# Turning token tiles once between an output projection and the FFN's up projection

## The chip, the cores and the metric

The kernel runs on one core of a Trainium2 chip. The metric is the device time of one execution in microseconds, the median of several runs. The core has five engines that run side by side and meet by semaphores: TensorE (PE in the profile; PEld is its weight load), VectorE (DVE), ScalarE (ACT), GpSimd (POOL) and SyncE (SP), whose queue issues most DMA transfers. Matmuls write to PSUM, which holds eight banks of 128 x 512 float32 numbers; VectorE and ScalarE read it, GpSimd works in SBUF.

## The reference

A trunk of two layers over 1024 tokens with 1024 features. Layer 0 mixes tokens by differential attention, layer 1 by multi-head latent attention; after each comes a gated MLP whose up projection passes through a causal convolution.

```python
for i in range(DEPTH):
    h = rms_norm(x, attn_norm_g[i])
    if i % N_MIXERS == 0:
        x = x + diff_attention(h, ...)      # ends in  o @ w_o
    else:
        x = x + mla_attention(h, ...)       # ends in  o @ w_o
    h = rms_norm(x, ffn_norm_g[i])
    x = x + conv_ffn(h, ffn_w_up[i], ffn_conv_w[i], ffn_conv_b[i], ffn_w_down[i])
return rms_norm(x, final_norm_g)

def conv_ffn(h, w_up, conv_w, conv_b, w_down):
    u = h @ w_up                            # 1024 x 5632
    c = causal depthwise conv of width 3 over u, plus conv_b
    g, val = jnp.split(c, 2, axis=-1)
    return (jax.nn.silu(g) * val) @ w_down
```

What matters here is the seam in each layer: `x + o @ w_o`, the norm of the sum, and the operands of `h @ w_up`.

## The kernel before

**Products in two parts.** Every float32 operand is split into an upper part in the fp32r format (`hi`, a ScalarE copy, line 127) and the remainder (`lo`, a subtraction on VectorE or GpSimd, line 130). A product is three matmuls (`mm3`, lines 119 to 121): upper by lower, upper by upper, lower by upper.

**Seven products instead of eight.** The up projection multiplies 2 x 2 blocks by a Strassen-Winograd scheme. For pair q the token tiles q and q + 4 give four blocks. B11 and B21 are the first and second feature halves of tile q, B12 and B22 those of tile q + 4. The scheme needs B11, B21, B22 and the sums T1 = B12 - B11, T2 = B22 - T1, T3 = B22 - B12 and T4 = B21 - T2. Weights have blocks A11, A12, A22 and sums S1 to S4. All seven token operands are needed with features on the partitions, so they are turned: four TensorE transposes of 128 x 128 into a PSUM bank (line 186), then an upper and a lower part read that bank (`turn_blocks`).

**The seam, `project_rest` (from line 623).** Eight token tiles come in the order 0, 4, 1, 5, 2, 6, 3, 7. Each tile multiplies the second half of the attention's output (loaded from DRAM by `project`, line 589, and split) with `w_o` into two PSUM banks, tag S, first 512 columns and then the rest, 24 matmuls each. VectorE adds the product to the tile (line 698), SP stores the sum for the later residual (`x_d`, line 699), ScalarE sums the squares (line 157), VectorE and GpSimd form the reciprocal root (lines 164, 167), and VectorE applies it and the gain in place (line 657), so this step also waits until the store has read the tile. The sums T1 to T4 are taken in token layout, mostly on GpSimd (lines 634 to 641), and turned afterwards like the blocks. `half` places the turns in the middle of a tile's matmuls, two tiles after the tile that they turn. What is left after tile 7 goes into the list `late`: one entry before each of the first products.

**The first products, in `up` (from line 748).** For the first of the 22 feature blocks, the products run on token halves of 256 columns in the order of `FIRST`: 14 products of 12 matmuls. `ORDER0` names the operands: A11 B11, A12 B21, S1 T1, S4 B22, S2 T2, S3 T3, A22 T4. Weight sums are made by `sum_of` (line 775), parts by `high`, `low` and `prepare`. Results wait in PSUM banks and are added up on VectorE (lines 864 to 874) and copied on ScalarE (line 862). From the second block on, products have 512 columns.

**What sets the order.** Inside `manual_schedule` the named engines run in the order in which the program is written: PE and DVE through the seam and the first products, ACT too from there on. All other queues (ACT, POOL and SP in the seam) are ordered by a planner that simulates the program. PSUM has two double banks (tag S), three single banks (tag b) and one (tag u). `halves(...)`, `units(...)` and `slots(...)` name places of 2, 4 and 8 KB per partition in SBUF.

Of the kernel before, what the change touches and what calls it, by code (L numbers as in the profile page):

```python
# [13 lines left out]
ALU = mybir.AluOpType  # L14
# [42 lines left out]
class Trunk:  # L57
# [526 lines left out]
    def project(self, i, ks, W, o_d, os, raw):  # L584

        nc = self.nc
        s = slice(i * P, (i + 1) * P)
        o = raw([P, 4, P])
        nc.sync.dma_start(o, o_d[ks[0] : ks[0] + 4, :, s].rearrange("k p s -> p k s"))
        oh, ol = (os([P, 4, P], F32R) for _ in range(2))  # L590
        self.hi(oh, o)
        self.lo(ol, o, oh, nc.gpsimd)
# [5 lines left out]
        return into  # L598

# [23 lines left out]
    def project_rest(self, W, o_d, os, X, at, x_d, g, junk, places, nat, more, begin):  # L623

        nc = self.nc
        T = {}
        sums = {}
        first, rest = slice(0, 512), slice(512, 1024)

        def sub(name, q, eng):  # L630
            a, b = (X[i] for i in self.PAIRS[q])
            if name == "T1":
                sums[q] = nat([P, 512])
                eng.tensor_sub(sums[q], b[:, first], a[:, first])
            elif name == "T2":
                eng.tensor_sub(sums[q], b[:, rest], sums[q])
            elif name == "T4":
                eng.tensor_sub(sums[q], a[:, rest], sums[q])
            else:
                sums["T3", q] = more([P, 512])  # L640
                eng.tensor_sub(sums["T3", q], b[:, rest], b[:, first])

        def turn(name, q):

            if name not in T:
                T[name] = [self.at(place, [P, 4, 512], F32R) for place in places[name]]
            a, b = (X[i] for i in self.PAIRS[q])
            src = {"B11": a[:, first], "B21": a[:, rest], "B22": b[:, rest], "T3": sums.get(("T3", q))}.get(name)
            if src is None:
                src = sums[q]  # L650
            s = slice(q * P, (q + 1) * P)
            self.turn_blocks(src, lambda part: T[name][part][:, :, s])

        v, gp = nc.vector, nc.gpsimd

        def norm(i):
            nc.vector.scalar_tensor_tensor(X[i], X[i], r.pop(i), g, ALU.mult, ALU.mult)
            if i >= 4:
                sub("T1", i - 4, v if i == 7 else gp)

        def turns(*which):
            for x in which:
                turn(*x)

        def half(n):

            if n < 2:
                return
            i = tiles[n - 2]
            q = i % 4  # L670
            if i < 4:
                turns(("B11", q), ("B21", q))
                if q:
                    turns(("B22", q - 1))
            else:
                turns(("T1", q))
                sub("T2", q, gp)
                if q == 0:
                    sub("T3", q, gp)

        tiles = [i for pair in self.PAIRS for i in pair]
        r = {}
        ready = self.project(tiles[0], range(4, 8), W, o_d, os, self.raw)
        region = ExitStack()
        region.enter_context(self.tc.manual_schedule(engines={mybir.EngineType.PE, mybir.EngineType.DVE}))
        for n, i in enumerate(tiles):
            into, y = ready, self.big()
            into(y[:, :512], 0)
            half(n)
            if n + 1 < NT:  # L690
                ready = self.project(tiles[n + 1], range(4, 8), W, o_d, os, self.raw)
            into(y[:, 512:], 512)
            if n == NT - 1:
                begin()
# [35 lines left out]

# [1212 lines left out]
```

## Time and profile before

| | |
|---|---|
| median of 3 runs | 2436.9 us (2436.48 to 2437.53) |
| span of the profiled execution | 2437.8 us |
| TensorE busy | 2366.7 us, 97% |
| VectorE busy | 1904.5 us, 78% |
| ScalarE busy | 1304.2 us, 53% |
| GpSimd busy | 628.4 us, 26% |
| seam and first products, layer 0 | 546.4 to 619.2 us |
| seam and first products, layer 1 | 1733.5 to 1808.2 us |

The profile shows one execution. No time is recorded for it beside its span, which stands 0.9 us above the median. Busy time of overlapping matmuls is counted once, and their ends are modelled. In rows of the timeline stand start, duration, engine, line, operation, output and inputs by name, and in brackets the idle time before and what ended it. In rows of the waits view stand who waited for whom, the total, the count and the longest. A "group" row has count, busy time and the mean in ns. The two rows of the table on the seam begin with the first matmul of the third token tile and end with the first product of 512 columns.

### The profile page before, as it was taken

To read this page: it belongs to the slowest core of one execution; us is meant where nothing else is said; L and a number is where in the kernel's file an instruction comes from. 1 tells how busy PE (TensorE), PEld (TensorE's weight loads), DVE (VectorE), ACT (ScalarE), POOL (GpSimd) and SP (SyncE) were. 2 spreads that over 40 slices of the span, in tenths; PEclk is the share of its full clock that TensorE was granted. 3 is DMA by queue.
4 is the path that set the end of the run, shared out by engine and by line. 5 is a ranking of instruction groups with operands and counts; after the bars stand their busy time and mean duration, and the time that the engine had idled before them with its cause. 6 is when DMAs were issued, how large, how long until landed. Compare 5 with 4: busy or idle time off the path is not lost. (4 is left out here: it accounts for less than half of the span.)

```text
span 2437.8 us, 32825 instructions
## 1 busy us (share of the span) xinstructions
PE 2366.7 (97%) x12032; PEld 2010.7 (82%) x12032; DVE 1904.5 (78%) x3094; ACT 1304.2 (53%) x2434; POOL 628.4 (26%) x500
## 2 busy tenths in 40 slices
PE   7999999999999999999999999999999999999998
PEld 6888787888888888878898789988888888887886
DVE  6667776856888888899864788886478888888997
ACT  5677777844444444444444777775344444443444
POOL 4545454425000000000042666664330000000001
PEclk9999999999999999999999999999999999999999
DMA  4101101233222222553222111123312222227502
GB/s 161 44 33 42 35 36 44 100 100 126 70 78 82 83 82 91 199 171 116 84 89 61 62 40 40 40 88 109 104 70 87 80 93 79 78 86 276 169 5 78
DMA packets 95793, 213.93 MB, mean 88 GB/s; under 512 B 8720, under 2 KB 33936, under 8 KB 95632
## 3 DMA queue, kind: packets, MB, share of 16 engines
q1 hardware_dynamic: 86448, 184.04, 22.5%
q10 hardware_dynamic: 9184, 27.79, 3.1%
q8 instruction: 95, 1.56, 0.3%
q14 instruction: 66, 0.54, 0.1%
HBM read 159.37 MB, written 52.43 MB: 87 GB/s over the span
## 5 line engine op out<-in xcount | busy, mean ns | idle before, releaser
L167 POOL TENSOR_TENSOR st<-st,mhalf 128x1 f32<-128x1 f32 x56 | 36.2, 648 | 1315.7 <-DVE st L164 1310.7
L127 ACT CAST u<-h 128x512 fp32r<-128x512 f32 (+2 forms) x242 | 146.0, 619 | 279.7 <-DVE h L775 259.8
L119 PE MATMUL S<-s,u 128*128 128x512 f32 (+1 forms) x752 | 286.1, 380 | 0.6 <-DVE s L130 0.5
L120 PE MATMUL S<-s,u 128*128 128x512 f32 (+1 forms) x752 | 284.5, 378 | 0.0
L121 PE MATMUL S<-s,u 128*128 128x512 f32 (+1 forms) x752 | 284.5, 378 | 0.0
L119 PE MATMUL b<-s,u 128*128 128x512 f32 x588 | 230.6, 392 | 2.1 <-DVE S L1631 1.0
L121 PE MATMUL b<-s,u 128*128 128x512 f32 x588 | 229.0, 390 | 0.0
L120 PE MATMUL b<-s,u 128*128 128x512 f32 x588 | 229.0, 389 | 0.0
L832 DVE SCALAR_TENSOR_TENSOR u<-u,conv,u 128x1023 f32<-128x1023 f32 (+1 forms) x176 | 224.8, 1277 | 1.9 <-ACT u L828 1.9
L149 POOL TENSOR_TENSOR u<-u,st 128x384 f32<-128x384 f32 (+7 forms) x160 | 169.6, 1070 | 149.2 <-DVE st L1639 107.2
L119 PE MATMUL u<-s,s 128*128 128x512 f32 (+1 forms) x440 | 177.9, 404 | 13.4 <-ACT h L556 7.1
L127 ACT CAST s<-u 128x512 fp32r<-128x512 f32 (+2 forms) x202 | 128.8, 673 | 103.4 <-PE u L121 37.6
L130 DVE TENSOR_TENSOR u<-b,u 128x512 fp32r<-128x512 f32 (+1 forms) x256 | 158.0, 630 | 29.6 <-ACT u L127 27.9
L121 PE MATMUL u<-s,s 128*128 128x512 f32 (+1 forms) x440 | 172.6, 392 | 0.0
L120 PE MATMUL u<-s,s 128*128 128x512 f32 (+1 forms) x440 | 172.2, 391 | 0.0
L119 PEld LDWEIGHTS S<-s,u 128*128 128x128 f32 x752 | 142.0, 189 | 27.7 <-DVE s L130 0.9
L120 PEld LDWEIGHTS S<-s,u 128*128 128x128 f32 x752 | 142.0, 189 | 26.3
L121 PEld LDWEIGHTS S<-s,u 128*128 128x128 f32 x752 | 141.9, 189 | 26.1
L127 ACT CAST u<-b 128x512 fp32r<-128x512 f32 (+1 forms) x256 | 133.6, 550 | 36.6 <-PE b L252 27.4
L835 ACT ACTIVATE u<-u 128x1024 f32<-128x1024 f32 x44 | 46.8, 1063 | 187.5 <-DVE u L832 187.5
L130 DVE TENSOR_TENSOR u<-h,u 128x512 fp32r<-128x512 f32 x166 | 114.1, 687 | 32.4 <-ACT u L127 31.5
L130 DVE TENSOR_TENSOR s<-u,s 128x512 fp32r<-128x512 f32 (+2 forms) x187 | 127.5, 715 | 12.0 <-ACT s L127 11.8
(263 smaller groups left out, 6645.3 us busy)
## 6 DMA issues: line engine op xcount, KB each, us to landing
u<-in_ffn_up SPq DMA_DIRECT2D x88, 512.0 KB, 3.9
g_d<-u ACTq DMA_DIRECT2D x44, 512.0 KB, 2.6
u<-in_ffn_down SPq DMA_DIRECT2D x66, 256.0 KB, 4.9
u<-g_d SPq DMA_DIRECT2D x62, 256.0 KB, 3.8
s<-in_da_wqkv SPq DMA_DIRECT2D x23, 512.0 KB, 3.2
x_d<-u SPq DMA_DIRECT2D x16, 512.0 KB, 2.9
s<-x_d SPq DMA_DIRECT2D x8, 1024.0 KB, 10.7
u<-o_d SPq DMA_DIRECT2D x24, 256.0 KB, 2.8
```

The costliest lines, as they stand in the source:

```text
L119: mm(out, lh, rl, start=first, stop=False, skip_group_check=onto)
L120: mm(out, lh, rh, start=False, stop=False, skip_group_check=onto)
L121: mm(out, ll, rh, start=False, stop=last, skip_group_check=onto)
L127: self.nc.scalar.copy(out, src)
L130: (eng or self.nc.vector).tensor_sub(out, src, hi.bitcast(F32))
L149: self.nc.gpsimd.tensor_mul(x, x, s.to_broadcast(list(x.shape)))
L167: nc.gpsimd.tensor_tensor(r, s, self.mhalf, ALU.pow)
L832: nc.vector.scalar_tensor_tensor(t[half][:, back:], u[half][:, : S - back], w, t[half][:, back:], ALU.mult, ALU.add)
L835: nc.scalar.activation(t[0], t[0], AF.Silu)
```

## The change

- Each token tile is turned once, in its two halves: 16 sets of four transposes per layer instead of 28. The turn of a tile stands at the start of the matmuls of the tile after the next, and no longer in the middle. Tile 3 is turned after tile 7's matmuls, tile 7 before the fourth of the first products.
- B12 stays as a turned block too. ScalarE copies it to SBUF, and T1 to T4 are taken in the turned layout by VectorE, from the PSUM banks of the blocks and from one another. T1 gets a place of its own, T2, T3 and T4 overwrite the normed tiles. Their upper and lower parts are made from SBUF. Lower parts of T1 are made on GpSimd, and of T2 where the text says `gp`.
- A tile's add, squares and norm follow one tile later in the order of the text, during the next tile's matmuls. Loads of the attention's output are issued two tiles ahead.
- Tile 7 is added, squared and normed in halves of 512 columns; the normed halves go to two places of their own (h12, h13).
- GpSimd runs in written order too, until the first products end. Weight parts of the first block are made at named points (`start.part`), the third on VectorE, the fourth lower part on GpSimd.
- The list `late` has parts instead of turns. The two layers differ in what is made early: `("T1",)` in layer 0, `("T1", "T2", "B22")` in layer 1.

```diff
-    def project(self, i, ks, W, o_d, os, raw):
...
+    def project_load(self, i, ks, o_d, raw):
+        o = raw([P, 4, P])
         s = slice(i * P, (i + 1) * P)
+        self.nc.sync.dma_start(o, o_d[ks[0] : ks[0] + 4, :, s].rearrange("k p s -> p k s"))
+        return o
+
+    def project_parts(self, o, ks, W, os):
+        oh, ol = (os([P, 4, P], F32R) for _ in range(2))
+        self.hi(oh, o)
+        self.lo(ol, o, oh, self.nc.gpsimd)
...
-    def project_rest(self, W, o_d, os, X, at, x_d, g, junk, places, nat, more, begin):
+    def project_rest(self, W, o_d, os, X, at, x_d, g, junk, places, sums, early, begin):
...
+        def turn(i):
+            names = ("B11", "B21") if i < 4 else ("B12", "B22")
+            for name, cols in zip(names, (first, rest)):
+                ps = banks[name, i % 4] = self.bank("u" if name == "B22" else "b")
+                x = normed(i, cols)
+                for k in range(4):
+                    nc.tensor.transpose(ps[:, k * P : (k + 1) * P], x[:, k * P : (k + 1) * P], self.ident)
...
+        def copy(q):
+            tmp["B12", q] = sums([P, 512])
+            nc.scalar.copy(tmp["B12", q], banks["B12", q])
+
+        def sub(name, q):
+            x, y = {
+                "T1": lambda: (tmp["B12", q], banks["B11", q]),
+                "T3": lambda: (banks["B22", q], tmp["B12", q]),
+                "T2": lambda: (banks["B22", q], tmp["T1", q]),
+                "T4": lambda: (banks["B21", q], tmp["T2", q]),
+            }[name]()
+            if name == "T1":
+                tmp[name, q] = sums([P, 512])
+            else:
+                tmp[name, q] = normed(*{"T2": (q, first), "T3": (q + 4, first), "T4": (q + 4, rest)}[name])
+            dve.tensor_sub(tmp[name, q], x, y)
...
+        outer.enter_context(self.tc.manual_schedule(engines={mybir.EngineType.PE, mybir.EngineType.DVE}))
+        inner.enter_context(self.tc.manual_schedule(engines={mybir.EngineType.Pool}))
         for n, i in enumerate(tiles):
+            into, ys[n] = ready, self.big()
+            before = tiles[n - 1] if n else None
+            older = tiles[n - 2] if n > 1 else None
+            if older is not None:
+                q, a_tile = older % 4, older < 4
+                turn(older)
+            into(ys[n][:, first], 0)
+            into(ys[n][:, rest], 512)
+            load(n + 2)
+            if n + 1 < NT:
+                ready = parts(n + 1)
+            else:
+                start = begin()
+            if before is None:
+                continue
+            X[before] = X[before], at(before, X[before])
+            add(before, ys[n - 1])
+            store(before)
+            if older is not None:
+                if a_tile:
+                    high("B11", q)
+                else:
+                    copy(q)
+                    if q or "B22" in early:
+                        high("B22", q)
+            s = self.squares(X[before], junk)
+            if older is not None:
+                if a_tile:
+                    high("B21", q)
+                    if older == 1 and "B22" not in early:
+                        both("B22", 0)
+                    low("B11", q)
+                else:
+                    sub("T1", q)
+                    sub("T3", q)
+            r[before] = self.root(s, D)
             if n == NT - 1:
+                start.part(0)
+            if older is not None:
+                if a_tile:
+                    low("B21", q)
+                else:
+                    both("T1", q, gp)
+                    if q or "B22" in early:
+                        low("B22", q)
+                    sub("T2", q)
+                    if q < 2:
+                        sub("T4", q)
+                    if "T2" in early:
+                        both("T2", q, gp)
+            dve.scalar_tensor_tensor(X[before], X[before], r.pop(before), g, ALU.mult, ALU.mult)
+
+        y = ys[NT - 1]
+        turn(3)
+        X[7] = X[7], at(7, X[7])
+        add(7, y, first)
+        s1 = self.squares(X[7][1][:, first], junk[:, first])
+        start.part(1)
+        dve.tensor_scalar(s1, s1, 1.0 / D, EPS, ALU.mult, ALU.add)
+        add(7, y, rest)
+        s2 = self.squares(X[7][1][:, rest], junk[:, rest])
+        store(7)
+        start.sum("S1")
+        sub("T4", 2)
+        high("B11", 3)
+        r7 = self.root(s2, D, s1)
+        start.part(2, dve)
+        for cols, place in ((first, "h12"), (rest, "h13")):
+            ends[cols.start] = self.at(place, [P, 512])
+            dve.scalar_tensor_tensor(ends[cols.start], X[7][:, cols], r7, g[:, cols], ALU.mult, ALU.mult)
+        high("B21", 3)
+        if "T2" not in early:
+            both("T2", 0, gp)
+            both("T2", 1, gp)
+        low("B11", 3)
+        low("B21", 3)
...
         late = [
+            steps(),
+            steps(),
+            steps((copy, 3), (high, "B22", 3), (sub, "T1", 3), (both, "T1", 3, gp), (sub, "T3", 3), (low, "B22", 3), now=lambda: turn(7)),
+            steps((sub, "T2", 3), (sub, "T4", 3)),
+            steps((both, "T3", 0), (both, "T4", 0)),
+            steps(*(() if "T2" in early else ((both, "T2", 2),)), (both, "T3", 1)),
+            steps((both, "T2", 3), (both, "T4", 1)),
+            steps((both, "T3", 2), (both, "T3", 3)),
+            steps((both, "T4", 2)),
+            steps((both, "T4", 3)),
         ]
...
     def up(...)
-        prepare(1)
-        sum_of(0, "S1")
-        sum_of(0, "S2")
-        high(2)
-        low(2)
-        T, late, region = yield
+        def part(n, eng=None):
+            high(n)
+            low(n, eng or nc.gpsimd)
+
+        T, late, region, inner = yield SimpleNamespace(part=part, sum=lambda name: sum_of(0, name))
...
-        bank = dict(S1=one[:, first], S3=one[:, rest], A22=two[:, first], S4=two[:, rest], A12=two[:, first])
+        bank = dict(A11=one[:, rest], S1=one[:, first], S3=one[:, rest], A22=two[:, first], S4=two[:, rest], A12=two[:, first])
...
-                low(3)
+                low(3, nc.gpsimd)
...
+        inner.close()
         region.enter_context(self.tc.manual_schedule(engines={mybir.EngineType.Activation}))
```

Here `high` and `low` in `project_rest` make the upper and the lower part of a token operand, `both` makes the two, `add` and `store` are the residual sum and its store, and `steps` makes one entry of `late`.

More of the change, by code (lines that the diff above doesn't have):

```diff
@@ L661, in turns @@
[L661 to L674, printed above, removed]
-            else:
[L676 to L681, printed above, removed]
@@ L703, in project_rest @@
[L703 to L726 removed]
+            return T[name][part][:, :, q * P : (q + 1) * P]
```

114 lines of the change are left out of this document (43 added, 71 removed).

## The prediction

> **What bounds the kernel now.** I read the page first, then the windows view, PE's waits and the timeline around the change. The first rows are from the page and its chain of work.
>
> ```profile
> span 2437.8 us, 32825 instructions
> PE 2366.7 (97%) x12032; PEld 2010.7 (82%) x12032; DVE 1904.5 (78%) x3094; ACT 1304.2 (53%) x2434; POOL 628.4 (26%) x500
> PE 37%; DVE 2%; DMA 2%; issue 1%; POOL 1%; ACT 1%; SPq 0%; POOLq 0%; DVEq 0%; ACTq 0%
> ```
>
> TensorE is busy nearly throughout and the chain names it before any other engine. So a change pays if it takes work from TensorE or closes a hole in it. The windows view has one row per layer for the stretch that is rewritten, from the first matmul of the third token tile to the first full-width product of the next FFN block; a third row is the latent attention between the two.
>
> ```profile
> 546.39:619.19 72.80, 68.92 (x425) 61.87 (x424) 50.68 (x66) 33.27 (x59) 38.68 (x34) 0.95 0.32 105
> 1733.50:1808.20 74.70, 68.96 (x425) 61.09 (x424) 49.72 (x66) 33.32 (x59) 38.83 (x34) 0.95 0.29 103
> 1270.00:1650.00 380.00, 370.69 (x2329) 331.65 (x2329) 279.61 (x675) 269.79 (x600) 219.98 (x179) 1.00 0.18 56
> ```
>
> Columns: span, then busy time (instructions) of PE, PEld, DVE, ACT, POOL, then PE's clock, DMA share, GB/s. The clock is 0.95 in both rewritten stretches. PE's waits there, layer 0 first and then the longest two of layer 1:
>
> ```profile
> PE b L186 <- DVE h L634: 3.5, 1, 3.5
> ...
> PE b L186 <- POOL h L634: 3.1, 1, 3.1
> PE b L186 <- DVE h L634: 2.1, 1, 2.1
> ```
>
> The turns of T1 wait for the subtraction that makes T1 (L634). The timeline gives TensorE's unit prices, and what follows the 3.1 us hole:
>
> ```profile
> 546.39 0.39 PE L119 MATMUL S<-s,h 128*128 128x512 f32 x1
> 549.12 1.03 PE L186 MATMUL b<-ident,u 128*128 128x128 f32 x8
> 549.91 0.48 PE L119 MATMUL S<-s,h 128*128 128x512 f32 x1
> 550.22 0.40 PE L120 MATMUL S<-s,h 128*128 128x512 f32 x1
> ...
> 618.14 0.28 PE L119 MATMUL S<-s,u 128*128 128x256 f32 x1
> 619.10 0.28 PE L121 MATMUL S<-s,u 128*128 128x256 f32 x1
> ...
> 1771.25 1.12 PE L186 MATMUL b<-ident,h 128*128 128x128 f32 x4 [3.10 <-POOL h L634]
> 1772.59 0.63 PE L120 MATMUL S<-s,h 128*128 128x512 f32 x1
> 1773.02 0.63 PE L121 MATMUL S<-s,h 128*128 128x512 f32 x1
> 1777.14 0.28 PE L119 MATMUL u<-s,u 128*128 128x256 f32 x1
> ```
>
> From 546.39 to 549.12 stand 12 matmuls of 512 columns, 0.2275 us each. Eight transposes take 0.79 us and stretch the next step from 0.23 to 0.31: 0.87, or 0.109 each. Eight steps of 256 columns take 0.96, 0.12 each. After the hole a 512-column step is 0.43.
>
> **TensorE's work.** A stretch holds 144 wide matmuls (32.8 us), 168 narrow ones (20.2) and 112 transposes (12.2): 65.2 us. So layer 0 has 7.6 us of holes and slow clock, layer 1 has 9.5. The change turns every token tile once: 16 sets of four instead of 28 per layer, 64 transposes (7.0 us). That leaves 60.0, and takes 5.2 us per layer straight off the path. With no hole left the stretches would save 12.8 and 14.7.
>
> **The first turn.** It moves from the middle of the third tile to its start. The chain to it, by store, add, root and norm of tile 0:
>
> ```profile
> 541.15 1.22 DVE L698 TENSOR_TENSOR u<-s,S 128x1024 f32<-128x1024 f32 x1 [4.22 <-PE S L121]
> 542.40 0.33 SPq L699 DMA_DIRECT2D x_d<-u  x1
> 543.59 0.15 DVE L164 TENSOR_SCALAR st<-st 128x1 f32<-128x1 f32 x1 [1.22 <-ACT u L157]
> 543.82 0.55 POOL L167 TENSOR_TENSOR st<-st,mhalf 128x1 f32<-128x1 f32 x1 [0.85 <-DVE st L164]
> 545.47 1.28 DVE L657 SCALAR_TENSOR_TENSOR u<-u,st,u 128x1024 f32<-128x1024 f32 x1 [1.73 <-DMA x_d<-u]
> ```
>
> The norm overwrites its tile, so it waits for the store, and ends at 546.75; TensorE is free at 546.39. With about 0.1 to release: a hole of 0.5 us per layer, bounded by 0 and the 2.73 of the half tile that covered it.
>
> **The tile loop.** A tile now lasts 12 × 2 × 0.2275 + 0.87 = 6.33 us on TensorE, and the next turn needs the previous tile's norm by its end. All subtractions move to VectorE and read PSUM; lower parts of T1 (and early T2) go to GpSimd. Prices:
>
> ```profile
> L130 DVE TENSOR_TENSOR s<-b,s 128x512 fp32r<-128x512 f32 x28 | 18.5, 686 | 11.5 <-ACT s L127 11.3
> 550.37 1.29 DVE L130 TENSOR_TENSOR s<-b,s 128x512 fp32r<-128x512 f32 x2 [1.05 <-ACT s L127]
> 602.13 0.59 ACT L127 CAST s<-b 128x512 fp32r<-128x512 f32 x1 [2.83 <-PE b L186]
> x_d<-u SPq DMA_DIRECT2D x8, 512.0 KB, 2.9
> u<-in_ffn_up SPq DMA_DIRECT2D x6, 512.0 KB, 4.0
> x_d<-u SPq DMA_DIRECT2D x1, 512.0 KB, 4.4
> u<-in_ffn_up SPq DMA_DIRECT2D x1, 512.0 KB, 5.0
> ```
>
> The DMA rows are the medians of layer 0 with their counts, then its last store (588.1) and a weight fetch of layer 1 (1760.5). Half-tile VectorE operations follow each other every 0.61. After a second-half tile, counted from TensorE's start: add 0.25 to 1.45; T1 and T3 to 2.7 (ScalarE's copy of B12 is done by 1.3); root at 3.1, since ScalarE's copy, upper part and squares end at 3.05; lower B22, T2 and T4 to 5.1; norm 6.3. That is on time by a hair, so I take 0.1 of hole for each of three such tiles. After a first-half tile the add, two lower parts and the root end at 3.9, but the norm waits for the store: 1.5 + 3.1 + 1.28 = 5.9. No hole. GpSimd now runs in written order, and each power stands behind the next tile's operand part; that part is done 2.1 us into the tile, before the root. The SP queue adds no hole: each store follows one load of operands whose buffer GpSimd frees about 2 us into the tile before. Where the first FFN weights are split, ScalarE's two casts stand ahead of its upper parts and squares and wait for a fetch (4.0 us). Layer 0 can fetch one tile earlier, and I take 0.2. In layer 1 two fetches and a store share the DMA engines in the last two tiles. I take the slow rows, 4.4 for that store and 5.0 for the fetch: 1.0 for tile 6's turn and 1.2 for tile 3's, 2.2 in all. Bounds for either layer: 0, and 3.1 by the hole that the same queue made before.
>
> **The last tile.** GpSimd and VectorE hold each other up, as the timeline shows:
>
> ```profile
> 592.57 1.28 POOL L130 TENSOR_TENSOR u<-u,u 128x512 fp32r<-128x512 f32 x1 [0.71 <-ACT u L127]
> 592.65 2.27 DVE L657 SCALAR_TENSOR_TENSOR u<-u,st,u 128x1024 f32<-128x1024 f32 x1 [1.43 <-DMA x_d<-u]
> 594.00 2.04 POOL L130 TENSOR_TENSOR u<-u,u 128x512 fp32r<-128x512 f32 x1 [0.16 <-ACT u L127]
> 594.96 1.63 DVE L634 TENSOR_TENSOR h<-u,u 128x512 f32<-128x512 f32 x1
> ...
> 582.20 0.69 DVE L130 TENSOR_TENSOR s<-b,s 128x512 fp32r<-128x512 f32 x1 [1.18 <-ACT s L127]
> 582.56 1.28 POOL L636 TENSOR_TENSOR h<-u,h 128x512 f32<-128x512 f32 x1
> ```
>
> An operation with both inputs in SBUF takes 2.27 instead of 1.28 and ends just after GpSimd's; they alternate. One with an input in PSUM keeps its 0.69. After the last tile's matmuls TensorE has the turn of tile 3 and three narrow products, 0.87 + 4.3 = 5.2 us, before tile 7's turn. Counted from the last tile's end: VectorE adds the first half, waits for its squares (behind ScalarE's cast of B11, which waits for tile 3's turn) until 2.1, adds the rest, forms S1, T4 of pair 2 and the root by 4.3, the power ends at 4.9. S1's upper part is ready at 4.3, its lower at 4.9, so the third product loses about 0.7. In layer 0 GpSimd's written order puts two T2 parts right behind the power; the two half norms alternate with them and end near 6.8 and 8.5, so tile 7's turn loses 2.0. In layer 1 those parts are done, but the casts of T3 and T4 delay ScalarE by as much. I take 2.7 for both; bounds 0 and the 3.5 of the old hole.
>
> **The first products.** S4's upper part is cast only after the evicted A11, and its lower part follows on GpSimd, 1.28 later: the product of S4 loses 1.7 in layer 0, 1.5 in layer 1. Behind it VectorE has about 27 half operations (16.5 us), ten of them lower parts of T2, T3 and T4 from SBUF that meet four or five GpSimd operations of 1.28. TensorE has 11 narrow products, 15.8 us, and overtakes it at T3 and T4 of pair 3: 2.5 in layer 0, 1.9 in layer 1. Bounds 0 and 6.4 (five times 1.28, nothing hidden).
>
> **The rest.** The planner reorders the latent attention between the stretches, same instructions. TensorE idles 9.3 us of 380 there; between minus 9.3 and plus 9.3 I take 0. What the FFN loop does behind the stretch keeps its order.
>
> **Sum.** Layer 0 holes: 0.5 + 0.5 + 2.7 + 1.7 + 2.5 = 7.9, stretch 60.0 + 7.9 = 67.9 against 72.8, gain 4.9. Layer 1: 0.5 + 0.3 + 2.2 + 2.7 + 1.5 + 1.9 = 9.1, 69.1 against 74.7, gain 5.6. Together 10.5. The profiled span 2437.8 becomes 2427.3; it stands 0.9 above the median of 2436.9, so the time is 2426.4, say 2426.
>
> **Rivals.** *The holes mostly close.* VectorE's order fits and GpSimd meets mainly operations that read PSUM: 5 us of holes in both layers together instead of 17.0 gives 2414. For it: every wait I add is a difference of two long chains. Against it: at 592 to 597 us the two engines met four times running.
>
> *The slow clock returns.* If tile 7's turn waits 3.1 us instead of 2.0, TensorE drops to 0.43 a step: the four transposes and 12 matmuls from 1771.25 to 1777.14 took 5.9 us instead of 3.2. Per layer 1.1 + 2.7, so 7.6 more: 2434, no measurable change. The 2.1 us hole of layer 1 was not followed by slow steps, so the limit lies between. The Trainium skill's page "TensorE: Matmul & The Clock Gate" (section "What's actually happening") gives halved clock after an idle window of about 3.4 us, in windows that run free of the kernel. By that rule holes of 2 us cost only themselves, and the sum stays at 2426; 0.43 against 0.2275 agrees with the halving, the 3.1 us hole with windows of which a little activity may be part.
>
> *Slower: the store is the loop.* The norm waits for its store, and the turn now follows one tile later with no half tile in between. With the 5 us landing seen below, the chain is 0.25 + 1.22 + 5.0 + 1.28 + 0.1 = 7.85 against 6.33, 1.5 us for each of 12 turns: 18 instead of the 3.0 counted in the loop, which ends at 2441. It decides from a landing near 4.6 us, 1.1 lost per turn. For and against it, two stores of layer 0 by the DMA view, at 547.9 and 580.0:
>
> ```profile
> x_d<-u SPq DMA_DIRECT2D x1, 512.0 KB, 3.0
> x_d<-u SPq DMA_DIRECT2D x1, 512.0 KB, 5.0
> ```
>
> The median was 2.9.
>
> **How the numbers follow.** I give the forecast 0.50, closed holes 0.20, the slow clock 0.14, the store loop 0.16. A measurement of this kernel tells about 0.2% (4.9 us), so 2432 to 2442 is no change. The forecast's own range is 2420 to 2434, a tenth of it no change, and the attention's order spreads every case: faster 0.66, same 0.18, slower 0.16. For 8 in 10 the range runs from 2412 to 2440.
>
> **What would show it.** PE should list 11936 instructions, 96 fewer. The waits of T1's turn on L634 vanish and the clock in both stretches rises to about 1. New rows should show turns waiting for a VectorE norm, about 0.5 at tile 0 and 2 at tile 7, and narrow products waiting for GpSimd and VectorE lower parts. The stretches should last about 68 and 69 us. I am wrong if they last under 64 or over 72, or if the attention gains or loses more than 4.

## The result and the profile after

The changed kernel takes 2430.35 us in the median of 12 runs (2428.16 to 2432.78), the kernel before 2435.84 us beside it (12 runs, 2434.5 to 2437.53). The ratio is 0.9979, with a 95% interval of 0.9971 to 0.9986: faster by 5.5 us, about half of the forecast 10.5, and inside the range. The profiled execution took 2430.68 us.

The page of the kernel after, in the rows that answer to those of before:

```profile
span 2428.9 us, 32660 instructions
PE 2355.0 (97%) x11936; PEld 1997.5 (82%) x11936; DVE 1916.0 (79%) x3111; ACT 1305.3 (54%) x2446; POOL 618.5 (25%) x489
```

TensorE issues 96 instructions fewer and is busy 11.7 us less; VectorE is busy 11.5 us more. The windows view of the kernel after has the two rewritten stretches, then the FFN of layer 0 from the end of its stretch to its first store of `x_d`, and the latent attention from that store to the third tile of layer 1:

```profile
548.80:617.84 69.04, 63.32 (x377) 55.48 (x377) 56.76 (x75) 34.13 (x64) 31.79 (x26) 0.98 0.33 111
1735.15:1802.95 67.80, 61.73 (x377) 54.10 (x377) 53.92 (x74) 34.07 (x64) 34.63 (x27) 1.00 0.34 113
617.84:1210.19 592.35, 587.27 (x2589) 485.64 (x2588) 512.63 (x720) 257.49 (x396) 2.56 (x2) 1.00 0.31 105
1210.19:1735.15 524.96, 514.48 (x3122) 456.89 (x3121) 365.87 (x826) 334.18 (x733) 275.84 (x223) 1.00 0.22 69
```

The stretches are 69.0 and 67.8 us where 67.9 and 69.1 were forecast, 136.8 instead of 137.0 in sum. Against 72.8 and 74.7 in the profile of before that is 10.7 us, and yet the medians differ by 5.5 only. So either something between the seams gives a part back, or the profile of before showed longer stretches than that kernel usually has. The first runs below test these two as theories A and B.

TensorE's waits in the stretch of the kernel after, layer 0 first (instructions and who ended the wait; total, count, longest), then layer 1:

```profile
PE S L119 <- ACT s L127: 2.6, 1, 2.6
PE u L660 <- DVE h L782: 1.1, 1, 1.1
PE b L660 <- DVE h L782: 0.8, 1, 0.8
PE b L660 <- DVE u L763: 0.6, 2, 0.4
PE S L119 <- DVE u L695: 0.5, 1, 0.5
...
PE S L119 <- DVE u L941: 2.6, 1, 2.6
PE b L660 <- DVE u L763: 1.5, 2, 1.3
PE S L119 <- DVE u L695: 1.0, 1, 1.0
PE S L119 <- DVE s L130: 0.8, 1, 0.8
```

L660 is a turn, L763 the norm of a tile, L782 that of half of tile 7, L695 the add of tile 7's second half, L941 an add in the first products. The long waits of T1's turn are gone, and in their place stand many short ones and one of 2.6 us in each layer. The timeline of the kernel after, around tile 7's two turns and that long wait:

```profile
595.16 0.66 PE L660 MATMUL b<-ident,h 128*128 128x128 f32 x4 [0.76 <-DVE h L782]
596.92 0.63 PE L660 MATMUL u<-ident,h 128*128 128x128 f32 x4 [1.11 <-DVE h L782]
600.28 0.28 PE L121 MATMUL S<-s,u 128*128 128x256 f32 x1
603.16 0.55 PE L119 MATMUL S<-s,u 128*128 128x256 f32 x1 [2.60 <-ACT s L127]
603.51 0.41 PE L120 MATMUL S<-s,u 128*128 128x256 f32 x1
606.28 0.28 PE L121 MATMUL S<-s,u 128*128 128x256 f32 x1
...
602.34 0.68 DVE L941 TENSOR_TENSOR u<-S,u 128x512 f32<-128x512 f32 x1
1788.05 0.68 DVE L941 TENSOR_TENSOR u<-S,u 128x512 f32<-128x512 f32 x1
1788.87 0.36 PE L119 MATMUL S<-s,u 128*128 128x256 f32 x1 [2.60 <-DVE u L941]
```

The product of S4 starts 0.14 us after VectorE's add of A12 (L941) in both layers: 602.34 + 0.68 = 603.02 and 603.16, 1788.73 and 1788.87. That add reads the other half of the PSUM tile into which S4's product goes. The profile names a ScalarE cast in layer 0 and the add in layer 1, so whether that add is what is waited for is left to an experiment.

Below, a stretch runs, as here, from the moment when TensorE is done with the second tile's matmuls to the first product of 512 columns. In the old seam that is the start of the third tile's first matmul; in the new one the wait for the first turn and the turn itself come first. A stretch without a hole would take 60.0 us, by the counts of the prediction.

### The profile page after: what moved, and what is told of

Same layout as the page of the kernel before. It is cut to its first block, busy times and chain, and to the rows that moved or that the text cites. A ratio compares the mean times of both kernels' runs of the same rounds, so it can differ in the third digit from the quotient of the medians.

```text
span 2428.9 us, 32660 instructions
## 1 busy us (share of the span) xinstructions
PE 2355.0 (97%) x11936; PEld 1997.5 (82%) x11936; DVE 1916.0 (79%) x3111; ACT 1305.3 (54%) x2446; POOL 618.5 (25%) x489
## 4 chain that ended last, share of the span: by engine, by line
PE 82%; DVE 7%; ACT 5%; DMA 3%; issue 2%; POOL 1%; SPq 0%; DVEq 0%; POOLq 0%; ACTq 0%
PE S L119 13%; PE S L121 13%; PE S L120 13%; PE b L119 8%; PE b L120 8%; PE b L121 8%; PE u L119 4%; PE u L120 4%; PE u L121 4%; PE b L252 3%; DMA u<-g_d 2%; PE u L1727 1%; DVE s L130 1%; PE u L1726 1%; ACT s L127 1%
## 5 line engine op out<-in xcount | busy, mean ns | idle before, releaser
L119 PE MATMUL S<-s,u 128*128 128x512 f32 (+1 forms) x768 | 290.5, 378 | 7.6 <-ACT s L127 2.6
L121 PE MATMUL S<-s,u 128*128 128x512 f32 (+1 forms) x768 | 289.5, 377 | 0.1
L120 PE MATMUL S<-s,u 128*128 128x512 f32 (+1 forms) x768 | 289.4, 377 | 0.0
L127 ACT CAST s<-u 128x512 fp32r<-128x512 f32 (+2 forms) x230 | 145.0, 666 | 108.2 <-PE u L121 35.8
L130 DVE TENSOR_TENSOR u<-b,u 128x512 fp32r<-128x512 f32 (+1 forms) x256 | 157.4, 629 | 29.4 <-ACT u L127 28.0
L119 PEld LDWEIGHTS S<-s,u 128*128 128x128 f32 x768 | 145.2, 189 | 35.1 <-ACT s L127 5.5
L121 PEld LDWEIGHTS S<-s,u 128*128 128x128 f32 x768 | 145.2, 189 | 26.6 <-DVE u L130 0.5
L120 PEld LDWEIGHTS S<-s,u 128*128 128x128 f32 x768 | 145.3, 189 | 26.1
L130 DVE TENSOR_TENSOR s<-u,s 128x512 fp32r<-128x512 f32 (+2 forms) x210 | 150.0, 746 | 12.4 <-ACT s L127 12.2
L130 DVE TENSOR_TENSOR u<-h,u 128x512 fp32r<-128x512 f32 x164 | 112.7, 687 | 32.5 <-ACT u L127 31.5
```

The lines of the kernel that those rows point to most:

```text
L119: mm(out, lh, rl, start=first, stop=False, skip_group_check=onto)
L120: mm(out, lh, rh, start=False, stop=False, skip_group_check=onto)
L121: mm(out, ll, rh, start=False, stop=last, skip_group_check=onto)
L127: self.nc.scalar.copy(out, src)
L130: (eng or self.nc.vector).tensor_sub(out, src, hi.bitcast(F32))
```

## The experiments

There were eleven runs. Times are medians. A ratio is to the kernel before as it ran on the same chip beside it: 2434.38 us for the first four (27 runs), 2435.05 for the next four (33 runs), 2433.9 for the last three (9 runs).

### Both kernels again, and the seam in one layer alone

Two runs repeat the kernels without an edit. The two others give one layer the old seam, with its own `project` and first products:

```diff
-        operands = k.project_rest(
+        operands = k.project_rest_old(
```

> The kernel before, unchanged, for a second profile. Seam stretches of the first profile: 72.8 us in layer 0 and 74.7 in layer 1, each with one wide hole (3.5 and 3.1 us) followed by about 2.7 us of half-speed steps. Theory A (the reordered attention eats the gain): the same stretches again, within 0.5 us. Theory B (the first profile of before was a slow execution, because the half-speed steps do not follow the holes each time): at least one stretch is 1.5 to 2.7 us shorter and steps behind its hole keep about 0.23 us.

> The changed kernel, unchanged, for a second profile and more timings. Both theories: about 5 us below the kernel before, 2430 to 2431. Theory A: seam stretches 69.0 and 67.8 again within 0.5. Theory B: layer 0 about 1.2 us shorter when the steps behind its 2.6 us hole keep 0.12, layer 1 up to 1.2 longer when they do not.

> The new seam in layer 0, the old one in layer 1; the attention between them then runs in the changed kernel's order. Theory A (seams save 3.8 and 6.9 us, the reordered attention gives about 5 back): slower than before by about 1 us, 2437. Theory B (attention costs nothing, seams save less than the profile of before says): faster by 2 to 3, 2433.

> The old seam in layer 0, the new one in layer 1; all work before layer 1's seam runs in the old order. Theory A: faster by 6 to 7, 2429. Theory B: faster by 3 to 4, 2432.

Times: before again 2435.26 us (one run); after again 2430.41, ratio 0.9985 (0.9976 to 0.9993); layer 0 alone 2434.14, ratio 0.9998 (0.9989 to 1.0007); layer 1 alone 2429.53, ratio 0.9981 (0.9972 to 0.999). The windows view of before again gives the two stretches and the latent attention, that of after again the two stretches:

```profile
547.54:619.40 71.86, 67.94 (x425) 60.52 (x424) 50.42 (x66) 33.29 (x59) 38.72 (x34) 0.98 0.32 107
1734.16:1807.07 72.91, 68.17 (x426) 60.63 (x425) 50.09 (x66) 33.34 (x59) 38.70 (x34) 0.98 0.30 106
1210.57:1734.16 523.59, 513.84 (x3123) 458.45 (x3122) 366.38 (x826) 335.89 (x733) 275.88 (x223) 0.99 0.22 69
```

```profile
550.99:619.80 68.81, 62.22 (x377) 54.15 (x377) 56.92 (x75) 34.14 (x64) 31.84 (x26) 1.00 0.33 111
1735.76:1803.65 67.89, 61.73 (x378) 54.09 (x377) 53.95 (x74) 34.08 (x64) 34.66 (x27) 1.00 0.33 113
```

The stages of all six profiles, in us (the attention and FFN columns run from mark to mark as in the section above; old or new order of TensorE ahead of layer 1 in brackets):

| run | stretch, layer 0 | FFN | latent attention | stretch, layer 1 |
|---|---|---|---|---|
| before | 72.8 old | 590.9 | 523.4 (before's) | 74.7 old |
| before again | 71.9 old | 591.2 | 523.6 (before's) | 72.9 old |
| layer 1 alone | 71.4 old | 591.1 | 523.4 (before's) | 68.4 new |
| layer 0 alone | 68.7 new | 591.5 | 524.2 (after's) | 72.2 old |
| after again | 68.8 new | 591.8 | 524.1 (after's) | 67.9 new |
| after | 69.0 new | 592.4 | 525.0 (after's) | 67.8 new |

The old seam takes 72.0 and 73.3 us in the mean of three profiles, the new one 68.9 and 68.0: gains of 3.2 and 5.3, 8.4 in all (unrounded). Between the seams the new kernel loses 0.9 us in the FFN and 1.0 in the attention, again by means of three. The sum, 8.4 less 1.8 (unrounded), is 6.6, near the 5.5 and 4.0 us of the medians. The match is rough: in these six profiles what stands ahead of layer 0's stretch took 544.8 to 551.0 us, and what follows layer 1's 625.6 to 629.6, with no clear order by old and new seam. Both theories hold a part. The larger is that the profile of before showed its stretches longer than the others did (147.5 us, against 144.8 in before again). The reordered attention takes 1.0, not the 5 that would have explained all. Layer 1 alone is as fast as both together, and layer 0 alone can't be told from the kernel before; its 3.2 us may be partly spent in the stages that follow, but 1.8 us is as much as one stage of the same code scatters (the FFN takes 591.3 to 594.5 us in all the profiles with the new seam in layer 0).

One forecast of theory B failed in a telling way. In after again the steps behind layer 0's long wait kept 0.12 us, as B asked, and the stretch should have been 1.2 us shorter. It was 0.2 shorter (68.8 for 69.0): near its end stands a wait for VectorE of 1.1 us, where the first profile has a hole of 0.3.

```profile
PE S L119 <- DVE s L130: 1.1, 1, 1.1
```

### The PSUM tile that S4 shares

```diff
-bank = dict(A11=one[:, rest], ..., A12=two[:, first])
+bank = dict(A11=two[:, first], ..., A12=one[:, rest])
```

> Edit: the PSUM halves of A11 and A12 change places, so that S4's product shares its two-bank tile with A11 and no longer with A12, whose two adds on VectorE end 0.14 us before that product starts in both layers of the kernel after (603.02 to 603.16, 1788.73 to 1788.87). Theory P (the product of S4 waits for VectorE's adds of A12, because they hold the same tile): its hole of 2.9 us ends when GpSimd has S4's own lower part, which in the kernel after was at 602.15 in layer 0; the hole falls to 1.7 to 2.0 us in both layers, the half-speed steps behind it in layer 0 go (1.1 us), and the two stretches become 67.0 (from 69.0) and 66.9 (from 67.8): some 2 to 3 us of the total. Rival G (S4's own parts are what is late, as I had forecast): the hole stays at 2.6 to 2.9 us and the total stays within 1 us of the kernel after. The planner orders the attention anew after this edit, so the verdict goes by the hole and the two stretches, the total can move by 2 us either way through that.

2436.51 us, ratio 1.001 (1.0 to 1.002). TensorE's waits in layer 0, then both stretches and the attention:

```profile
PE S L119 <- DVE s L130: 1.9, 2, 1.1
...
PE S L121 <- POOL u L130: 0.8, 1, 0.8
...
PE S L119 <- ACT u L127: 0.3, 1, 0.3
```

```profile
550.45:619.42 68.97, 62.85 (x378) 54.34 (x377) 56.80 (x75) 34.11 (x64) 31.83 (x26) 1.00 0.33 111
1744.93:1812.99 68.06, 62.32 (x377) 54.24 (x377) 54.04 (x74) 34.17 (x64) 34.73 (x27) 1.00 0.35 113
1213.88:1744.93 531.05, 516.56 (x3123) 458.69 (x3121) 366.41 (x826) 335.79 (x733) 275.39 (x223) 0.99 0.22 68
```

The hole ahead of S4's product falls from 2.8 us (603.16 less 600.28 and one step of 0.12) to 1.1 us of waits, 0.3 for S4's upper part on ScalarE and 0.8 for the lower on GpSimd; with the stretched steps beside them it is 1.5. So theory P is right on the hole, and wrong on the stretches, which stay at 69.0 and 68.1: near the end stand 1.9 us of waits for VectorE's lower parts (L130), where the kernel after had a hole of 0.3. The total is worse for another reason, the attention: 531.1 us instead of 524 to 525. The profiled execution was this run's longest (2442.75 us); the run without lower parts, below, shows the same attention, 531.2 us, in an execution of 2427.48.

### Tile 7's second add first

```diff
-        dve.tensor_scalar(s1, s1, 1.0 / D, EPS, ALU.mult, ALU.add)
         add(7, y, rest)
+        dve.tensor_scalar(s1, s1, 1.0 / D, EPS, ALU.mult, ALU.add)
```

> Edit: the second half of tile 7's add is issued on VectorE ahead of the operation on the sum of squares, which waits 1.3 us for ScalarE's squares in layer 0 of the kernel after. Theory V (VectorE's written order delays the add, and with it the product of the second pair's first half): the hole ahead of that product (0.5 us in layer 0, 1.0 in layer 1) goes to 0 to 0.2, the root of tile 7 and its half norms come 0.5 to 1.2 us earlier, and the holes ahead of tile 7's turns (0.8 and 1.1 in layer 0) become smaller by as much: 1 to 2 us in layer 0, 1 in layer 1, total 2428.5 or so. Rival S (the add's own input, the store of tile 7 or ScalarE's power, is what is late): the hole stays, only VectorE's wait changes its place, total as the kernel after, 2430.4.

2430.57 us, ratio 0.9986 (0.9977 to 0.9995). The waits for the add (L695) are gone in both layers, as theory V has it. The gain that it gave (1 to 2 us in layer 0, 1 in layer 1) did not come: the stretches are 68.4 and 67.8 us, in layer 0 0.6 less than in the kernel after, in layer 1 nothing, where a wait of 0.7 us for a weight part of GpSimd stands in place of the 1.0. By the total this cannot be told from the kernel after.

### GpSimd's T2 parts of layer 0 later

```diff
-        if "T2" not in early:
-            both("T2", 0, gp)
-            both("T2", 1, gp)
...
-steps((copy, 3), ..., (low, "B22", 3), now=lambda: turn(7)),
+steps((copy, 3), ..., (low, "B22", 3), (both, "T2", 0, gp), (both, "T2", 1, gp), now=lambda: turn(7)),
```

> Edit: the two lower parts of T2 that GpSimd makes in layer 0 beside tile 7's half norms are issued some 8 us later, in the last tile's second step; layer 1 is as it was. Theory A (GpSimd and VectorE take turns on SBUF there: half norms 3.44 us for two beside GpSimd's T2 parts in layer 0, 1.41 without them in layer 1): half norms 1.4 us, the holes ahead of tile 7's turns in layer 0 fall from 1.9 us in sum to 0.3 or less, and 1 to 1.9 us of it stays in the stretch of layer 0 (69.0 becomes 67.2 to 68), the rest is lost to T2's own sum coming later; total 2428.5 to 2429.5. Rival C (tile 7's turn waits for the chain of add, square and power, and the half norms are only its end): holes fall by less than 0.5 us, total 2430.4. Rival W (T2 late makes its own product wait): the holes ahead of the turns go and one of 1 to 2 us comes ahead of the products of T2, total 2430 to 2431.

2431.55 us, ratio 0.999 (0.9981 to 0.9999). VectorE's two half norms, first in the kernel after, then in this run, with two lower parts near the end of the stretch:

```profile
593.33 3.44 DVE L782 SCALAR_TENSOR_TENSOR h<-u,st,u 128x512 f32<-128x512 f32 x2 [0.44 <-POOL st L167]
...
592.78 1.41 DVE L782 SCALAR_TENSOR_TENSOR h<-u,st,u 128x512 f32<-128x512 f32 x2 [0.44 <-POOL st L167]
...
609.84 1.77 DVE L130 TENSOR_TENSOR s<-h,s 128x512 fp32r<-128x512 f32 x1
611.53 1.77 DVE L130 TENSOR_TENSOR s<-u,s 128x512 fp32r<-128x512 f32 x1
```

Beside GpSimd's parts the two half norms took 3.44 us in the kernel after; now they take 1.41, and tile 7's turns wait for nothing. Theory A is right there. But the stretch of layer 0 is 69.3 us, 0.3 longer: two waits for VectorE's lower parts, 1.8 us in sum, come at the end. Rival W described the course of it, with the place further back.

### All three together

The exchanged halves and the second add first, as above, with GpSimd's T2 parts right behind tile 7's store in place of later, and the sums of S2 and S4 ahead of the last root:

```diff
         store(7)
+        if "T2" not in early:
+            both("T2", 0, gp)
+            both("T2", 1, gp)
         start.sum("S1")
         sub("T4", 2)
+        start.sum("S2")
+        start.sum("S4")
         high("B11", 3)
         r7 = self.root(s2, D, s1)
         start.part(2, dve)
```

> Edits: A11 and A12 exchange halves; tile 7's second add ahead of the operation on the squares; GpSimd's T2 parts of layer 0 right behind the store of tile 7, ahead of the power; the sums of S2 and S4 on GpSimd ahead of the last root. If theories P, V and A all hold and VectorE's tail stays covered: holes of both stretches down by 3.5 to 5 us in layer 0 and 2.5 to 3.5 in layer 1, stretches 64.5 and 65, total 2423 to 2425. If the tail takes half of it back (VectorE's last sums then end the wait): stretches 66.5, total 2426 to 2428. If the rivals hold: 2430.

2430.12 us, ratio 0.9984 (0.9975 to 0.9993). The stretches are 69.3 and 67.5 us: nothing gained in layer 0. TensorE there, and a window of what follows:

```profile
591.82 0.28 PE L120 MATMUL S<-s,u 128*128 128x256 f32 x1
594.03 0.39 PE L121 MATMUL S<-s,u 128*128 128x256 f32 x1 [1.93 <-DVE u L130]
```

```profile
595.10:602.06 6.96, 6.25 (x31) 5.99 (x30) 6.17 (x9) 3.57 (x7) 3.07 (x3) 0.51 0.00 0
```

S1's lower part now stood too late on VectorE, and behind the 2.1 us that it cost the granted clock was halved for 6.8 us (a mean of 0.51 over 6.96 us). VectorE was no longer full: in this stretch it is busy 53.1 us, where the three runs above have 56.8 to 57.0. So here the hole and the slow clock behind it look like what ate the gain; two runs below, with 0.5 us in place of that hole and the full clock, are 2 to 3 us shorter there.

### VectorE's lower parts left out

The exchanged PSUM halves again, without the eight lower parts of T3 and T4 on VectorE. Their products take the upper part twice, so the output lacks the lower parts and counts the upper ones double.

```diff
+                if name in ("T3", "T4"):
+                    T[name][1] = T[name][0]
...
         def low(name, q, eng=dve):
+            if name in ("T3", "T4"):
+                return
```

> As the run with the exchanged PSUM halves (stretches 68.97 and 68.06 us, holes of 1.9 and 1.8 us at the end that wait for VectorE's lower parts), and the eight lower parts of T3 and T4 on VectorE of each layer are left out: the products read the upper part in their place, so TensorE's work is the same and the result is less exact. Theory E (holes in this stretch only change places because VectorE, busy 17.7 of the last 17.8 us of layer 0 in the kernel after, ends it): the two last holes go and no other takes their place, stretches 66.5 to 67.2 and 65.8 to 66.4. Rival Q (GpSimd's weight parts or TensorE's own chain end the stretch): 68.5 and 67.6, other holes of the same sum. The attention's order is that of the exchanged halves, so the total stays some 8 us above the kernel after, less the 2 to 4 us of the stretches.

2427.48 us (one run), where some 2434 to 2436 was expected. The attention takes its 531.2 us, but what stands ahead of layer 0's stretch, which the edit doesn't touch, takes 545.4 us for 548.8 in the kernel after. The windows view of the two stretches:

```profile
545.36:611.42 66.06, 62.02 (x377) 54.15 (x377) 50.33 (x67) 34.51 (x65) 31.11 (x26) 1.00 0.35 116
1733.99:1799.71 65.72, 61.85 (x377) 54.15 (x377) 48.50 (x66) 34.67 (x65) 34.54 (x27) 1.00 0.35 117
```

Against the run with exchanged halves the stretches fall by 2.9 and 2.3 us, with TensorE's work the same, and the waits for L130 at the end are gone. That is theory E, with 0.4 and 0.1 more than it gave. So VectorE's row of work does end the stretch of that kernel, and holes ahead of it had taken time that the last ones would have taken.

### S1's part and the T2 parts early, with the attention in two orders

Beside the exchanged halves and the second add first, both of these runs hold this edit; the second also exchanges `sub("T4", 2)` and `start.part(2, dve)`:

```diff
         store(7)
         start.sum("S1")
         sub("T4", 2)
+        start.part(2, dve)
+        if "T2" not in early:
+            both("T2", 0, gp)
+            both("T2", 1, gp)
         high("B11", 3)
         r7 = self.root(s2, D, s1)
-        start.part(2, dve)
         for cols, place in ((first, "h12"), (rest, "h13")):
...
+        start.sum("S2")
+        start.sum("S4")
```

> As the run with all three edits, with S1's lower part on VectorE ahead of GpSimd's T2 parts and of the root, and the sums of S2 and S4 behind the half norms, so that the third product no longer waits 2.1 us (layer 0) and 1.6 us (layer 1) for it. The attention's order is that of the kernel after but for six lines. Theory H (in the run with all three edits layer 0 lost its gain to 6.8 us of halved clock from 595 us on, behind the hole of 2.1 us): without that hole the steps stay at 0.12 us, stretch 65 to 66 in layer 0 and 65.5 to 66.5 in layer 1, total 2424 to 2426. Rival E (VectorE ends the stretch whatever is done ahead of it): the holes move behind tile 7's turn, stretches 68 and 67.3, total 2429 to 2431.

> As the run with early sums, with one subtraction (T4 of pair 2) and S1's lower part exchanged on VectorE: the seam should be within 0.5 us per layer of that run. What differs is the planner: it gives the latent attention a third order, 354 lines of TensorE's list away from the kernel after and 390 from the kernel before. From the first store of the FFN of layer 0 to the third tile of layer 1 the order of before took 523.4 us, that of after 524.0 to 525.0, that of the exchanged halves 531.1. If the order alone sets this time, the third order gives its own value, between 522 and 532, and the total follows it one for one; if the 7 us of the exchanged halves came from the seam, it is 524 here.

The first takes 2422.36 us (5 runs, 2421.23 to 2424.52), ratio 0.9954 (0.9941 to 0.9966); the second 2424.62 us, ratio 0.996 (0.9947 to 0.9974). Both are faster than both kernels of this document, though the second's interval just meets that of the kernel after; the first is also faster than its forecast of 2424 to 2426. The profiled span of the first is 6.2 us shorter than that of the kernel after (2422.7 and 2428.9), and the stretches hold 3.3 us of it; the rest lies in stages that the edit doesn't touch, and how much of it scatters is open. The first one's stretches, and VectorE in layer 0 of it:

```profile
547.04:613.60 66.56, 62.14 (x377) 54.18 (x377) 52.37 (x75) 34.10 (x64) 31.89 (x26) 1.00 0.34 115
1728.49:1795.43 66.94, 61.91 (x377) 54.10 (x377) 53.30 (x74) 34.16 (x64) 33.94 (x27) 1.00 0.35 115
```

```profile
599.69 2.61 DVE L130 TENSOR_TENSOR s<-u,s 128x512 fp32r<-128x512 f32 x4
...
608.58 1.50 DVE L849 TENSOR_TENSOR h<-u 128x512 f32<-128x512 f32 x1 [2.67 <-DMA u<-in_ffn_up]
```

The clock is 1.00, tile 7's turns wait for nothing, and VectorE's four lower parts behind the add of A12 take 2.61 us where the kernel after needs 3.88, with a part of GpSimd beside them:

```profile
602.93 3.88 DVE L130 TENSOR_TENSOR s<-u,s 128x512 fp32r<-128x512 f32 x4
```

VectorE is busy 4.4 us less in layer 0 with the same 75 instructions, as fewer of them are lengthened beside GpSimd's, and the stretch is 2.5 us shorter. In layer 1 it is busy 0.6 us less, and the stretch is 0.9 shorter. Theory H holds for the clock, but the stretches came out 0.6 and 0.4 above its ranges. VectorE then runs dry for 2.67 us, waiting for the next block's weights. Whether that is the next limit is open: an earlier fetch was not tried, and TensorE waits only 0.6 us for VectorE behind it (at 612.06).

The latent attention, first that of the second of these runs, then the waits for VectorE's lower parts ahead of its turns (L252): before, after, exchanged halves, second run:

```profile
1207.35:1729.32 521.97, 512.48 (x3122) 456.99 (x3121) 366.45 (x826) 335.75 (x733) 276.02 (x223) 1.00 0.22 69
```

```profile
PE b L252 <- DVE u L130: 0.7, 2, 0.5
```

```profile
PE b L252 <- DVE u L130: 2.5, 4, 0.9
```

```profile
PE b L252 <- DVE u L130: 5.0, 10, 0.9
```

```profile
PE b L252 <- DVE u L130: 1.6, 3, 0.7
```

The expectation calls this a third order. By the traces it is none: between the two marks TensorE's matmuls stand, by line and tile names (buffer numbers aside), in the order of the kernel before but for three of 3121. (Most of the 390 lines then lie elsewhere; the seams of the two kernels differ.) The same instructions take 522.0 us here and 523.4 to 523.6 in the three runs with before's order, 523.6 to 525.0 in after's, and 531.1 and 531.2 in that of the exchanged halves. So orders that are the same but for a few lines spread by about 1.5 us, and the 1.0 between before and after is no more than that. The 7 us of the exchanged halves are far beyond it, and the first of these runs, which has the exchanged halves too but after's order save a few lines, takes 523.6. So those 7 us go with the order and not with the seam ahead. That the total follows the attention one for one did not show: the second run has the shorter attention by 1.6 us, stretches of 67.2 and 67.2 us, together 1.0 longer (in layer 0 0.7, where 0.5 was the bound), and a median 2.3 us above the other's, with intervals that overlap. Of the 7 us of the worst order these waits explain 2.5; the others were not traced singly.

## Why the prediction was right, and where it was off

**TensorE's work: right.** 11936 instructions, and the steps of the prediction's prices add up to 60.0 us in each new stretch.

**The holes: right in sum, partly wrong in place.** With the slow clock among them they are 9.0 us above 60.0 in layer 0 (forecast 7.9) and 7.8 in layer 1 (forecast 9.1). That both layers together come within 0.2 us of the forecast is partly luck: errors of 1.1 and 1.3 us cancel, and within a layer single terms were off by as much as 2.2.
- First turn: 0.4 us in both layers (548.80 to 549.22 in layer 0), for 0.5.
- Tile loop: 0.4 us at one turn of layer 0, for 0.5. In layer 1 tile 6's turn waits 1.3 us, for 1.0; tile 3's doesn't wait, for 1.2.
- Last tile, layer 0: tile 7's turns wait 0.8 and 1.1 us, for 2.0, by the alternation named; the run with T2 later confirms the cause. In place of the 0.7 at the third product stand 0.5 at the second, which needs the PSUM banks that tile 7's add reads. In layer 1 that wait is 1.0, and the 2.0 for the turn did not come.
- Product of S4: 2.8 us in both layers, for 1.7 and 1.5. I had followed only its weight parts. The add of A12 on the other half of its PSUM tile came later still; the exchange of the halves brought the hole to 1.5.
- VectorE's backlog: 0.3 and 0.8 us at the end, for 2.5 and 1.9. The long hole at S4 had given VectorE the time to catch up. With that hole shortened, the backlog showed with 1.9 and 1.8.
- One row was misread: the operation that "ends just after GpSimd's" ended 1.1 us after it (592.65 + 2.27 = 594.92 and 592.57 + 1.28 = 593.85). The forecast alternation came all the same, 3.44 us for two half norms.

The step that failed in method is to add holes of one chain as if each stood alone. With VectorE the last to finish, a hole ahead is paid out of the hole behind. In layer 0 the exchange of the halves took 1.3 us out of one place and T2 later took 1.9, and they changed the stretch by -0.1 and +0.3. The slow clock of 1.3 us in layer 0 is another such term: the second profile is free of it and 0.2 us shorter.

**The baseline: the term that was off.** I subtracted 10.5 us from one profiled execution and called its span 0.9 us above the median. In the profiled executions whose time is recorded, the time is 1.7 to 1.9 us above the span (after: 2430.68 and 2428.9). By that, before's took some 2439.6 us, 3.8 above its later median of 2435.84. The changed span was forecast at 2427.3 and came at 2428.9; the time was forecast 0.9 below the span and lies 1.8 above it. Those 1.6 and 2.7 us are the 4.3 between 2426.4 and the profiled 2430.68. So a part of the forecast gain was an accident of that execution: its stretches were 2.2 us longer than the mean of the three profiles with it, 3.3 longer than the mean of the others, and had the clock at 0.95, the others 0.98. What follows layer 1's stretch was long in it too, 629.6 us where the five others took 625.6 to 627.1.

**The attention: right in bounds.** I took 0 between minus and plus 9.3; it lost 1.0, and the FFN 0.9, of which I had counted nothing; both are near the scatter of the same code. That the exchange of two PSUM halves moved it by 7 us shows that the bounds were not too wide.

**The rivals.** The holes did not close: 16.8 us stayed. The store loop did not come about, 1.3 us at one turn of twelve. The slow clock returned in one of the two layers of the profile, behind the hole of 2.8 us, and stretched the steps there by 1.3 us (14 at 0.21 instead of 0.12); in the second profile of the same kernel it did not return.

## What to carry to other kernels

Sum up the row of work of the engine that ends a stage, collisions included, before pricing single waits: closing a wait pays only as far as that engine gets done sooner. Take the baseline from several executions of the stage, and with the clock that each had. And where a planner orders what follows, time the untouched stage after every edit, since its order may move by more than the edit is worth.

## What the runs showed of the hardware

The length of a hole didn't decide whether the clock was halved behind it. I had put the limit between 2.1 and 3.1 us. In before again it halved behind a hole of 1.8 us in layer 1, with eight transposes between:

```profile
1785.38 0.63 PE L186 MATMUL b<-ident,h 128*128 128x128 f32 x4 [1.77 <-DVE h L634]
...
1786.84 0.42 PE L120 MATMUL S<-s,u 128*128 128x256 f32 x1
```

The kernel after had it behind the hole of 2.8 us at S4 of layer 0, for 3.4 us; the second execution of the same kernel had the same hole and full speed:

```profile
602.84:606.24 3.40, 3.08 (x14) 3.11 (x15) 3.40 (x5) 0.23 (x1) 2.22 (x2) 0.50 0.00 0
```

```profile
605.11 0.35 PE L119 MATMUL S<-s,u 128*128 128x256 f32 x1 [2.60 <-ACT s L127]
605.31 0.28 PE L120 MATMUL S<-s,u 128*128 128x256 f32 x1
```

So holes of 2 to 3 us had no fixed price here; that it is a matter of when a hole comes fits these rows, but was not tested by shifting one. The slow phases seen in the seams lasted 3.4 us (after, before again) or 6.8 (all three together). The Trainium skill, page "TensorE: Matmul & The Clock Gate", section "What's actually happening", has the gate look at windows of about 3.4 us that run free of the kernel; lengths of one and two windows and the chance of it agree with that. It asks for an idle window, and here less was enough: of the 3.4 us ahead of the halving at 602.84 in the kernel after, the first third held matmuls (the last from 600.28 us, 0.28 long).

Engines that hold each other up on SBUF showed as longer operations and not as waits: two half norms took 3.44 us beside GpSimd's parts and 1.41 without them. The Trainium skill, page "SBUF — State Buffer", section "Who interferes with whom", states this contention for VectorE operations with two inputs in SBUF beside a GpSimd one that reads SBUF, and the runs agree.
